# Attention weights turned by transposing DMA transfers instead of by TensorE, in a one-core hybrid encoder step

## The chip, the cores and the metric

The kernel runs on one core of a Trainium2 chip. The metric is the device time in microseconds (us). A kernel's time is the median of several runs. The profile comes from one execution of its own, and its span runs from the first to the last instruction.

## The reference, cut to what matters

One layer of a streaming encoder over 2048 prompt positions (and 32 sample positions): a combined projection, a short convolution, differential attention with 4 heads, an output projection, an MLP and a gate. The part that the change touches is the attention of the prompt:

```python
s = jnp.einsum('bqhmd,bkhmd->bhmqk', qf, kf)            # m = 0, 1: two maps per head
s = jnp.where(visible, s + bias[None, :, None], NEG_INF)
a = jax.nn.softmax(s, axis=-1)
attn = a[:, :, 0] - lam * a[:, :, 1]
o = jnp.einsum('bhqk,bkhd->bqhd', attn, v.astype(f))
o = rmsnorm(o, g_subln) * (1.0 - lam_init)
```

A block of 128 queries sees the keys up to its own block, so query block `qb` (0 to 15) has `qb + 1` key blocks of 128.

## The kernel before, in words

Every product is done in fp16 parts: a number is split into a high and a low fp16 part (`split`: ScalarE writes the high part, VectorE the low one), and three products are summed.

After the input has been normalised and turned, the attention runs head by head. A head's work is cut into 16 units (`Unit`), one for each query block, in ascending order for heads 0 to 2 and in descending order for head 3. A unit's keys are cut into chunks of up to 512 (`TG`). A unit has two stages:

- `scores`: for each of the two maps and each chunk TensorE makes the scores in one of three PSUM tiles (`sc`, L587 and L588), VectorE adds the position bias and keeps a running maximum (L591), and when the row is whole ScalarE takes the exponential and its sum (L598). The results are the fp32 tiles `s0` and `s1`, of which four lie in SBUF, for two units.
- `values`: ScalarE scales `s1` (L622), VectorE adds the maps (L105, `s<-s,sg,s`), TensorE transposes each 128x128 block in fp32 into PSUM (L629, `pta`), `split` makes two fp16 parts of it in `at` (three buffers), and TensorE multiplies them by the values in three products a block (L616 to L618, into `smb`). `subnorm` normalises the result.

`weave` writes one step: the scores of unit u, then `values` of the unit before it, and between the points of both a number of steps of `fill`, which are other heads' projections, the convolution, the sample attention and, in the last seven units of head 3, the first output projections. A scheduler then orders each engine's instructions by these priorities and sets the waits. All DMAs are issued by SyncE (SP), in order, and a queue's instruction waits there for its data, its buffer and one of eight completion counters.

After the attention come the output projection, the MLP and the gate, which the change does not touch.

Of the kernel before, what the change touches and what calls it, by code (L numbers as in the profile page):

```python
# [17 lines left out]
P = 128  # L18
# [16 lines left out]
def hymba_step_kernel(  # L35
# [34 lines left out]
    def small_o():  # L70
        k = turn["o"] = turn["o"] + 1
        return smb[:, (k % 4) * P:(k % 4 + 1) * P]
# [411 lines left out]
    def all_of(gen):  # L484
        for _ in gen:
            pass


    def weights_of(z1, z2, k0, rows=P):

        r, d, sg, sgc = t1("rz"), t1("ca"), t1("sg"), t1("sgc")
        ts(G, d[:rows], z1[:rows], alam[:rows], MUL, z2[:rows], ADD)
        V.reciprocal(out=r[:rows], in_=d[:rows])
        ts(G, sgc[:rows], z1[:rows], r[:rows], MUL, nlam[:rows], MUL)
        G.tensor_tensor(out=sg[:rows], in0=z2[:rows], in1=r[:rows], op=MUL)
        kk = t1("kk")
        if k0 is not None:
            ts(G, kk[:rows], sg[:rows], z1[:rows], MUL, k0[:rows], MUL)
        else:
            G.tensor_tensor(out=kk[:rows], in0=sg[:rows], in1=z1[:rows], op=MUL)  # L500
        ts(G, kk[:rows], kk[:rows], kk[:rows], MUL, EPS, MUL)
        return sg, sgc, kk

    def subnorm(o, kk, out, rows=P):
        jk = pq.tile([P, P], F16, tag="jko", bufs=1, name="jko")
        ss = t1("sso")
        A.activation(out=jk[:rows], in_=o, func=AF.Square, accum_out=ss[:rows])
        r = t1("rso")
        ts(G, r[:rows], ss[:rows], 1.0 / P, MUL, kk[:rows], ADD)
        G.tensor_tensor(out=r[:rows], in0=r[:rows], in1=mhalf[:rows], op=ALU.pow)  # L510
        ts(V, out, o, r[:rows], MUL)

    def sample_attention(j):
# [52 lines left out]
        T.transpose(pt[:, :DS], ys, ident[:DS, :DS])  # L566
        split(yas_h[:, j, :], yas_l[:, j, :], pt[:, :DS], gsa)

    class Unit:


        def __init__(self, j, qb, idx):
            self.idx = idx
            self.j, self.qb, self.nk = j, qb, (qb + 1) * P
            self.chunks = [(c, min(TG, self.nk - c)) for c in range(0, self.nk, TG)]

# [24 lines left out]
                    yield  # L601

        def weigh(self):
            self.sg, self.sgc, self.kk = weights_of(self.z[0], self.z[1], heads[self.j]["k0"])

        def values(self):
            s1, s2 = self.s
            vhl = heads[self.j]["vhl"]
            po = small_o()
            nkb = self.qb + 1  # L610

            def av(c0, w_, at):
                for i in range(w_ // P):
                    kb = c0 // P + i
                    a_ = slice(i * P, (i + 1) * P)
                    T.matmul(po, at[:, 0, a_], vhl[:, 0, kb], start=(kb == 0), stop=False)  # L616
                    T.matmul(po, at[:, 0, a_], vhl[:, 1, kb], start=False, stop=False)
                    T.matmul(po, at[:, 1, a_], vhl[:, 0, kb], start=False, stop=(kb == nkb - 1))  # L618

            for c0, w_ in self.chunks:  # L620
                cs = slice(c0, c0 + w_)
                A.activation(out=s2[:, cs], in_=s2[:, cs], func=AF.Copy, scale=self.sgc)  # L622
                stt(s1[:, cs], s1[:, cs], self.sg, s2[:, cs], MUL, ADD)
            yield
            ats = []
            for c0, w_ in self.chunks:
                pt = ptp.tile([P, TG], F32, tag="tp", name="pta")
                for i in range(w_ // P):
                    T.transpose(pt[:, i * P:(i + 1) * P], s1[:, c0 + i * P:c0 + (i + 1) * P], ident)  # L629
                at = att.tile([P, 2, TG], F16, tag="at", bufs=3, name="at")  # L630
                split(at[:, 0, :w_], at[:, 1, :w_], pt[:, :w_], 2.0 ** 14)
                ats.append((c0, w_, at))
                yield
                if len(ats) > 1:
                    av(*ats[-2])
            if len(self.chunks) == 1:
                yield
            av(*ats[-1])
            qi = self.qb % 4
            if self.idx % 4 == 0:  # L640
                yg_of[0] = att.tile([P, 4, P], F32, tag="yg", bufs=1, name="yg")
            self.yg = yg_of[0]
            subnorm(po, self.kk, self.yg[:, qi, :])

        def store(self):
            if self.idx % 4 != 3:
# [364 lines left out]
    all_of(run_chunk(GV, 0))  # L1011
    all_of(proj_q(0, 0))
    ready(place[GB, 0])
    last = before = None

    def weave(u, last, fills, nfill):

        points = len(u.chunks) * 2 if u else 0
        if last:
            points += len(last.chunks) + 1 + (len(last.chunks) == 1)  # L1020
        state = {"p": 0, "f": 0}

        def step():
            state["p"] += 1
            while state["f"] < nfill * state["p"] // points:
                state["f"] += 1
                for f in fills:
                    next(f, None)
        if u:
            for _ in u.scores():  # L1030
                step()
        if last:
            last.weigh()
            for _ in last.values():
                step()
        while state["p"] < points:
            step()

    for j in range(NH):
        set_bias(j)  # L1040
        fill = between(j)
        done = 0

        for idx in range(S // P):

            qb = idx if j < NH - 1 else S // P - 1 - idx
# [17 lines left out]
            weave(u, last, [fill], want - done)  # L1064
            done = want
            if idx % 4 == 3 and qfill is not None:
                all_of(qfill)
            if before:
                before.store()
            before, last = last, u  # L1070
        if j < NH - 1:
            all_of(fill)
    weave(None, last, [fill], EARLY_STEPS - done)
    before.store()
    last.store()
    all_of(fill)
# [690 lines left out]
```

## Time and profile before

| | |
|---|---|
| median of 3 runs | 2599.41 us (2597.41 to 2602.86) |
| profiled execution | 2600.33 us, span 2598.6 us |
| mean granted TensorE clock | 0.988 of full speed |
| TensorE busy (matmuls) | 2520.6 us, 97% |
| VectorE busy | 1677.6 us, 65% |
| ScalarE busy | 1208.8 us, 47% |
| GpSimd busy | 689.7 us, 27% |
| attention, from the first position bias to the last unit | about 97 to 960 us |

The matmuls are pipelined, so their durations overlap: what one costs is the time to the start of the next. The shares are means over stages with different limits.

### The profile page before, as it was taken

To read this page: it belongs to the slowest core of one execution; us is meant where nothing else is said; L and a number is where in the kernel's file an instruction comes from. 1 tells how busy PE (TensorE), PEld (TensorE's weight loads), DVE (VectorE), ACT (ScalarE), POOL (GpSimd) and SP (SyncE) were. 2 spreads that over 40 slices of the span, in tenths; PEclk is the share of its full clock that TensorE was granted. 3 is DMA by queue.
4 is the path that set the end of the run, shared out by engine and by line. 5 is a ranking of instruction groups with operands and counts; after the bars stand their busy time and mean duration, and the time that the engine had idled before them with its cause. 6 is when DMAs were issued, how large, how long until landed. Compare 5 with 4: busy or idle time off the path is not lost.

```text
span 2598.6 us, 42548 instructions
## 1 busy us (share of the span) xinstructions
PE 2520.6 (97%) x16495; PEld 1343.5 (52%) x16495; DVE 1677.6 (65%) x2873; ACT 1208.8 (47%) x2126; POOL 689.7 (27%) x1299
## 2 busy tenths in 40 slices
PE   8998999999999989999999999999999999999998
PEld 7755755765575554444444444444444444444444
DVE  6567957757877866875665656555455447655764
ACT  5446745644765555553444344345333223334553
POOL 2132233123222243432322222220120102223442
PEclk9999999999999999999999999999999999999999
DMA  5121111112120224554444444446653457531221
GB/s 176 50 66 33 43 30 46 42 34 58 45 57 27 82 78 134 171 201 171 157 166 164 163 157 167 142 162 245 225 206 118 158 174 251 201 114 59 86 79 57
DMA packets 213595, 311.57 MB, mean 120 GB/s; under 512 B 19024, under 2 KB 109552, under 8 KB 213392
## 3 DMA queue, kind: packets, MB, share of 16 engines
q1 hardware_dynamic: 213392, 308.85, 35.8%
q8 instruction: 129, 2.11, 0.3%
q14 instruction: 74, 0.61, 0.1%
HBM read 206.68 MB, written 97.92 MB: 117 GB/s over the span
## 4 chain that ended last, share of the span: by engine, by line
PE 66%; DVE 4%; ACT 2%; DMA 2%; issue 2%; POOL 1%; DVEq 0%; POOLq 0%; SPq 0%; ACTq 0%
PE mm L1299 8%; PE mm L1301 7%; PE mm L1300 7%; PE mm L1530 6%; PE mm L1532 6%; PE mm L1531 6%; PE mm L894 4%; PE mm L896 4%; PE mm L898 4%; PE lin L315 1%; PE lin L314 1%; PE lin L313 1%; DMA wtmp<-in_w_pe_gate_dram 1%; DVE s L591 1%; PE ptr L185 1%
## 5 line engine op out<-in xcount | busy, mean ns | idle before, releaser
L1530 PE MATMUL mm<-v,hl 128*128 128x512 f16 x896 | 339.8, 380 | 3.4 <-ACT hl L1491 3.4
L1532 PE MATMUL mm<-v,hl 128*128 128x512 f16 x896 | 340.0, 380 | 3.0 <-DVE hl L1492 3.0
L1531 PE MATMUL mm<-v,hl 128*128 128x512 f16 x896 | 340.6, 380 | 0.0
L313 PE MATMUL lin<-uh,whl 128*128 128x512 f16 (+1 forms) x832 | 264.4, 332 | 3.9 <-DVE ks L105 3.5
L314 PE MATMUL lin<-ul,whl 128*128 128x512 f16 (+1 forms) x832 | 264.4, 332 | 1.4 <-DVE ul L105 1.2
L315 PE MATMUL lin<-uh,whl 128*128 128x512 f16 (+1 forms) x832 | 264.1, 332 | 0.0
L1491 ACT ACTIVATE hl<-fr 128x1024 f16<-128x1024 f32 x112 | 116.9, 1051 | 302.1 <-PE mm L1532 287.7
L1492 DVE TENSOR_TENSOR hl<-fr,hl 128x1024 f16<-128x1024 f32 x112 | 145.1, 1306 | 171.8 <-ACT hl L1491 169.1
L598 ACT ACTIVATE s<-s,nm 128x128 f32<-128x128 f32 (+15 forms) x128 | 153.6, 1200 | 135.0 <-POOL nm L100 134.5
L1299 PE MATMUL mm<-u,w 128*128 128x512 f16 x448 | 170.5, 381 | 1.1 <-ACT w L170 1.1
L1300 PE MATMUL mm<-u,w 128*128 128x512 f16 x448 | 170.4, 380 | 0.0
L1300 PE MATMUL mm<-u2b,w 128*128 128x512 f16 x448 | 169.8, 379 | 0.0
L1301 PE MATMUL mm<-u,w 128*128 128x512 f16 x448 | 169.5, 381 | 0.0
L1299 PE MATMUL mm<-u2b,w 128*128 128x512 f16 x448 | 169.2, 379 | 0.0
L1301 PE MATMUL mm<-u2b,w 128*128 128x512 f16 x448 | 168.5, 379 | 0.0
L591 DVE CUSTOM_DVE_ANT_0 s<-sc,bias,mx 128x512 f32<-128x512 f32 (+3 forms) x192 | 134.9, 703 | 19.9 <-PE sc L588 15.5
L1530 PEld LDWEIGHTS <-hl 128*128 128x128 f16 x896 | 87.8, 98 | 113.6 <-issue 6.8
L1532 PEld LDWEIGHTS <-hl 128*128 128x128 f16 x896 | 87.7, 98 | 111.0 <-DVE hl L1492 5.4
L1301 PEld LDWEIGHTS <-w 128*128 128x128 f16 x896 | 87.9, 98 | 105.7 <-issue 0.8
L1531 PEld LDWEIGHTS <-hl 128*128 128x128 f16 x896 | 87.8, 98 | 104.3 <-issue 1.5
L1299 PEld LDWEIGHTS <-w 128*128 128x128 f16 x896 | 88.9, 99 | 100.5 <-ACT w L170 1.2
L1300 PEld LDWEIGHTS <-w 128*128 128x128 f16 x896 | 87.9, 98 | 98.9 <-issue 0.8
(451 smaller groups left out, 5981.9 us busy)
## 6 DMA issues: line engine op xcount, KB each, us to landing
ff_d<-e SPq DMA_DIRECT2D x224, 256.0 KB, 2.1
fr<-ff_d SPq DMA_DIRECT2D x112, 512.0 KB, 4.6
raw<-in_w_down_dram SPq DMA_DIRECT2D x80, 512.0 KB, 4.9
xt<-in_x_prompt_dram SPq DMA_DIRECT2D x32, 512.0 KB, 4.3
stg<-in_w_up_dram SPq DMA_DIRECT2D x16, 1024.0 KB, 6.5
stgd<-in_w_down_dram SPq DMA_DIRECT2D x16, 1024.0 KB, 5.6
stg<-in_w_in_dram SPq DMA_DIRECT2D x24, 512.0 KB, 4.1
h_d<-ht SPq DMA_DIRECT2D x16, 512.0 KB, 2.9
```

The costliest lines, as they stand in the source:

```text
L313: T.matmul(o, w[:, 0, ft], rh[:, ft, c], start=(ft == 0), stop=False)
L314: T.matmul(o, w[:, 0, ft], rl[:, ft, c], start=False, stop=False)
L315: T.matmul(o, w[:, 1, ft], rh[:, ft, c], start=False, stop=(ft == FT - 1))
L591: V.tensor_tensor_reduce(out=s_[:, c0:c0 + w_], in0=ps[:, :w_], in1=bias[:, b0:b0 + w_], scale=h["idd"], scalar=-BIG if prev is None else ...
L598: A.activation(out=s_[:, :nk], in_=s_[:, :nk], func=AF.Exp, bias=nm, accum_out=zz)
L1299: T.matmul(o, w[:, c, 0, kt], x[:, :, 0, kt], start=first and kt == 0, stop=False, skip_group_check=True)
L1300: T.matmul(o, w[:, c, 0, kt], x[:, :, 1, kt], start=False, stop=False, skip_group_check=True)
L1301: T.matmul(o, w[:, c, 1, kt], x[:, :, 0, kt], start=False, stop=kt == 3, skip_group_check=True)
L1492: V.tensor_tensor(out=hl[:, 1], in0=fr, in1=hl[:, 0], op=SUB)
L1530: T.matmul(ps, hl[:, 0, u % 2, c], v[:, 0], start=(u == 0), stop=False)
L1531: T.matmul(ps, hl[:, 0, u % 2, c], v[:, 1], start=False, stop=False)
L1532: T.matmul(ps, hl[:, 1, u % 2, c], v[:, 0], start=False, stop=(u == NU - 1))
```

## The change

For 57 of the 64 units (heads 0 to 2, and the first nine of head 3) the weights are turned by DMA. VectorE adds the maps without a scaling by ScalarE ahead of it (`weights_apart` gives the ratio `r`, with one reciprocal more), `split` makes the two fp16 parts before the turn, in place of `s1`, and one transposing DMA for each chunk, issued by SP, writes both parts turned into `at`. The products with the values move from the step after the scores to the step after that, and are woven with the scores of that step. The last seven units of head 3 keep the old way (`turn_and_values`). The transfers' targets come from two tags: `q4`, which had so far been used only later, and `at`.

```diff
+    def weights_apart(z1, z2, k0):
+        rd, d, r, sg, rz = t1("rz"), t1("ca"), t1("sgc"), t1("sg"), t1("rz2")
+        V.reciprocal(out=rz, in_=z2)
+        ts(G, r, z1, rz, MUL, nlam, MUL)
+        ts(G, d, z1, alam, MUL, z2, ADD)
+        V.reciprocal(out=rd, in_=d)
+        ts(G, sg, z2, rd, MUL, 2.0 ** 14, MUL)
...
         def __init__(self, j, qb, idx):
             self.idx = idx
+            self.by_dma = j < NH - 1 or idx < FAST[j]
+            self.even = Unit.count % 2 == 0
...
+        def turn(self):
+            s1, s2 = self.s
+            self.ats = []
+            for i, (c0, w_) in enumerate(self.chunks):
+                cs = slice(c0, c0 + w_)
+                stt(s1[:, cs], s2[:, cs], self.r, s1[:, cs], MUL, ADD)
+                hl = s2[:, cs].bitcast(F16)
+                split(hl[:, :w_], hl[:, w_:], s1[:, cs], self.sg)
+                if i < 2 or self.even:
+                    if i % 2 == 0:
+                        two = pmix.tile([P, 2, NH, 2, P], F16, tag="q4", bufs=3, name="at2")
+                    at = two[:, i % 2].rearrange("p a b c -> p (a b) c")
+                else:
+                    at = att.tile([P, 2, TG], F16, tag="at", bufs=3, name="at")
+                    at = at.rearrange("p a (b c) -> p (a b) c", c=P)
+                n = w_ // P
+                nc.sync.dma_start_transpose(out=at[:, :2 * n, :], in_=hl)
+                self.ats.append((c0, w_, at[:, :n, :], at[:, n:2 * n, :]))
+                yield
+        def products(self, c0, w_, hi, lo):
...
         def values(self):
+            for a in self.ats:
+                self.products(*a)
+                yield
+            self.normed()
...
+    def weave(u, last, before, fill, nfill):
+        parts = []
+        if u:
+            parts.append((u.scores(), 2 * len(u.chunks)))
+        if before and before.by_dma:
+            parts.append((before.values(), len(before.chunks)))
         if last:
+            last.weigh()
+            if last.by_dma:
+                parts.append((last.turn(), len(last.chunks)))
+            else:
+                parts.append((last.turn_and_values(), len(last.chunks) + 1 + (len(last.chunks) == 1)))
+        points = sum(n for _, n in parts)
...
+        if u and before and before.by_dma:
+            (a, na), (b, nb) = parts[:2]
+            parts = parts[2:]
+            for k in range(na + 1):
...
```

Three places show how it moves instructions. The first is TensorE in a unit of head 1 with nine key blocks, before. `pta` is a turned block, `s` a map, `lin` a projection that fills:

```order
L617 LDWEIGHTS at
L617 MATMUL smb<-vhl,at 128x128
L618 LDWEIGHTS at
L618 MATMUL smb<-vhl,at 128x128
L629 MATMUL pta<-ident,s_6859 128x128
L379 LDWEIGHTS ul
L379 MATMUL lin<-whl,ul 128x128
L377 LDWEIGHTS uh
```

The same engine in head 1 of the changed kernel, where the products of a unit begin (`at_6376` is written by DMA; L655 to L657 are the three products):

```order
L313 LDWEIGHTS whl
L313 MATMUL lin<-uh,whl 128x512
L359 MATMUL ptk<-ident,kf 128x128
L655 LDWEIGHTS at_6376
L655 MATMUL smb<-vhl,at_6376 128x128
L656 LDWEIGHTS at_6376
L656 MATMUL smb<-vhl,at_6376 128x128
```

No turned block stands among TensorE's rows of these units any more: 516 of the 544 are gone, and the products wait for a DMA in their first row of a chunk.

The second place is VectorE where head 0 ends and head 1 begins, before. `s_4669` and `s_4718` are the maps of the last unit of head 0, `s_4950` and `s_5140` belong to the first two units of head 1:

```order
L591 ISA s_4950,mx<-sc,bias,idd_2972 128x128
L591 ISA mx 128x1
L105 SCALAR_TENSOR_TENSOR s_4669<-s_4669,sg,s_4718 128x512 x2
L105 SCALAR_TENSOR_TENSOR at<-pta,at 128x384
L105 SCALAR_TENSOR_TENSOR s_4669<-s_4669,sg,s_4718 128x512 x2
L493 RECIPROCAL rz<-ca 128x1
L591 ISA s_5140,mx<-sc,bias,idd_2972 128x256
```

The same place in the changed kernel. `s_4513` and `s_4574` are the maps of the last unit of head 0; the rows that write `s_4574` make the low fp16 parts which the DMA reads; `s_4950`, of the second unit of head 1, takes over the buffer of `s_4574`:

```order
L105 SCALAR_TENSOR_TENSOR s_4513<-s_4574,sgc,s_4513 128x512 x4
L572 RECIPROCAL rz_4931<-z_4779 128x1
L575 RECIPROCAL rz<-ca 128x1
L105 SCALAR_TENSOR_TENSOR s_4574<-s_4513,sg,s_4574 128x512 x2
L100 TENSOR_SCALAR yg<-smb,rso 128x128
L105 SCALAR_TENSOR_TENSOR s_4574<-s_4513,sg,s_4574 128x512
L105 SCALAR_TENSOR_TENSOR s_4762<-s_4772,sgc,s_4762 128x128
L105 SCALAR_TENSOR_TENSOR s_4574<-s_4513,sg,s_4574 128x512
L105 SCALAR_TENSOR_TENSOR s_4772<-s_4762,sg,s_4772 128x128
L610 ISA s_4940,mx<-sc,bias,idd_2941 128x256
L610 ISA mx 128x1
L610 ISA s_4950,mx<-sc,bias,idd_2941 128x256
```

The low part is made from SBUF now instead of from PSUM, and the score row that writes `s_4950` has to wait for the transfers that read `s_4574`: the last of them can be issued only four rows earlier. This is the shortest such distance; within a head it is mostly 20 to 40 rows.

The third place is the queue of SP in head 1, before (`stg` are weights on their way in, `qs` the queries' parts, `cz`, `mixc_d` and `ya_d` results on their way out):

```order
L422 DMA qs<-qs 64x512
L424 DMA qs<-qs 64x512
L421 DMA qs<-qs 64x512
L423 DMA qs<-qs 64x512
L463 DMA out_dram<-cz 128x2x1
L464 DMA out_dram<-czs 128x2x1
L654 DMA ya_d<-yhl 128x4x256
```

The same queue, changed:

```order
L645 DMA_TRANSPOSE at_5687<-s_5468 128x8x128
L645 DMA_TRANSPOSE at_5687<-s_5468 128x4x128
L463 DMA out_dram<-cz 128x2x1
L464 DMA out_dram<-czs 128x2x1
L704 DMA ya_d<-yhl 128x4x256
L461 DMA mixc_d<-yt 128x512
L521 DMA sbig<-in_cache_k_dram 128x2x128
L522 DMA sbig<-in_cache_v_dram 128x2x128
L645 DMA_TRANSPOSE at_5844<-s_5612 128x8x128
L645 DMA_TRANSPOSE at_5844<-s_5612 128x6x128
```

The queue gains 150 rows, one to four for each unit, and they stand among the loads and stores that were there before.

## Rows read from the trace of the kernel before

**Rows 1.** The page, part 1: busy time, share of the span, instructions.
```profile
PE 2520.6 (97%) x16495; PEld 1343.5 (52%) x16495; DVE 1677.6 (65%) x2873; ACT 1208.8 (47%) x2126; POOL 689.7 (27%) x1299
```

**Rows 2.** Busy time in four stretches, one for each head.
```profile
core 0: us, PE busy (x) PEld busy (x) DVE busy (x) ACT busy (x) POOL busy (x), PEclk, DMA share, GB/s
97.00:315.00 218.00, 207.39 (x1980) 140.53 (x1978) 155.18 (x369) 123.73 (x240) 59.34 (x172) 0.99 0.18 51
315.00:526.00 211.00, 202.31 (x1691) 127.86 (x1688) 153.04 (x369) 117.47 (x229) 62.19 (x179) 0.98 0.14 39
526.00:742.00 216.00, 207.74 (x1713) 128.98 (x1711) 158.49 (x376) 117.68 (x231) 61.19 (x177) 0.98 0.18 49
742.00:960.00 218.00, 200.23 (x1537) 120.72 (x1534) 171.04 (x390) 125.06 (x240) 67.04 (x180) 0.98 0.18 56
sum 863.00, PE 817.67 PEld 518.09 DVE 637.76 ACT 483.94 POOL 249.76; mean PE 204.42 PEld 129.52 DVE 159.44 ACT 120.98 POOL 62.44
```

**Rows 3.** Waits of TensorE from 97 to 960 us: total, times, longest.
```profile
PE sc L587 <- DVE mx L591: 17.6, 20, 2.2
PE smb L616 <- ACT at L170: 4.0, 4, 1.5
PE smb L618 <- DVE at L105: 4.0, 6, 1.9
...
PE pta L629 <- DVE at L105: 1.3, 2, 1.0
...
PE pta L629 <- DVE s L105: 1.0, 1, 1.0
```

**Rows 4.** The group of TensorE's transposes: busy, mean ns; idle before.
```profile
L629 PE MATMUL pta<-ident,s 128*128 128x128 f32 x544 | 87.8, 280 | 5.0 <-DVE yhl L105 2.3 <-DVE at L105 1.3 <-DVE s L105 1.0
```

**Rows 5.** Timeline of TensorE around four transposes: start, duration.
```profile
274.19 0.22 PE L379 MATMUL lin<-whl,ul 128*128 128x128 f16 x1
274.25 0.61 PE L629 MATMUL pta<-ident,s 128*128 128x128 f32 x4
274.69 0.22 PE L377 MATMUL lin<-whl,uh 128*128 128x128 f16 x1
```

**Rows 6.** Groups of VectorE, shapes kept apart.
```profile
L105 DVE SCALAR_TENSOR_TENSOR s<-s,sg,s 128x512 f32<-128x512 f32 x112 | 80.5, 745 | 20.8 <-ACT s L622 18.1 <-POOL cz L433 1.4 <-POOL nm L100 1.1
L105 DVE SCALAR_TENSOR_TENSOR at<-pta,at 128x512 f16<-128x512 f32 x112 | 75.4, 682 | 2.4 <-ACT at L170 1.9
L105 DVE SCALAR_TENSOR_TENSOR v<-raw,swd,v 128x512 f16<-128x512 f32 x96 | 72.6, 797 | 3.2 <-ACT v L170 3.2
...
L493 DVE RECIPROCAL rz<-ca 128x1 f32<-128x1 f32 x64 | 10.2, 159 | 31.4 <-POOL ca L102 30.9
```

**Rows 7.** Groups of ScalarE, shapes kept apart.
```profile
L622 ACT ACTIVATE s<-s,sgc 128x512 f32<-128x512 f32 x112 | 74.3, 715 | 38.6 <-POOL sgc L102 38.1
L170 ACT ACTIVATE at<-pta 128x512 f16<-128x512 f32 x112 | 64.3, 590 | 39.5 <-PE pta L629 36.9 <-PE smb L618 1.6
...
L170 ACT ACTIVATE v<-raw,swd 128x512 f16<-128x512 f32 x96 | 63.4, 709 | 44.3 <-DVE raw L1470 25.0 <-DVE raw L1461 14.3 <-DMA raw<-in_w_down_dram 4.8
```

**Rows 8.** DMA issues by tile: count, KB each, median us to landing.
```profile
ff_d<-e SPq DMA_DIRECT2D x224, 256.0 KB, 2.1
...
u2b<-u_d SPq DMA_DIRECT2D x5, 1024.0 KB, 11.1
...
qs<-qs SPq DMA_DIRECT2D x64, 64.0 KB, 1.9
...
out_dram<-cz SPq DMA_DIRECT2D x4, 1.0 KB, 8.6
```

**Rows 9.** Timeline of SP in head 0: start, time to issue.
```profile
268.62 0.38 SPq L391 DMA_DIRECT2D out_dram<-vt  x1
269.58 0.47 SPq L422 DMA_DIRECT2D qs<-qs  x1
```

**Rows 10.** Busy time at the end of head 0, columns as in rows 2.
```profile
260.00:325.00 65.00, 64.71 (x783) 51.82 (x782) 58.84 (x140) 50.76 (x94) 19.23 (x55) 1.00 0.16 43
```

**Rows 11.** The same stretch, transposes of L629 alone: us, PE, PEld.
```profile
260.00:325.00 65.00, 10.87 (x70) 7.62 (x69) 1.00 0.16 43
```

More of the change, by code (lines that the diff above doesn't have):

```diff
@@ L603, in weigh @@
         def weigh(self):
+            if self.by_dma:
+                self.sg, self.r, self.kk = weights_apart(self.z[0], self.z[1], heads[self.j]["k0"])
+                return
             self.sg, self.sgc, self.kk = weights_of(self.z[0], self.z[1], heads[self.j]["k0"])
-        def values(self):
-            s1, s2 = self.s
[L608 to L618, printed above, removed]
+        def turn(self):
[17 more added lines that the diff above has]
+                yield
@@ new lines, in products, with normed @@
+        def products(self, c0, w_, hi, lo):
+            vhl = heads[self.j]["vhl"]
+            if c0 == 0:
+                self.po = small_o()
+            for i in range(w_ // P):
+                kb = c0 // P + i
+                T.matmul(self.po, hi[:, i, :], vhl[:, 0, kb], start=(kb == 0), stop=False)
+                T.matmul(self.po, hi[:, i, :], vhl[:, 1, kb], start=False, stop=False)
+                T.matmul(self.po, lo[:, i, :], vhl[:, 0, kb], start=False, stop=(kb == self.qb))
+        def normed(self):
+            if self.idx % 4 == 0:
+                yg_of[0] = att.tile([P, 4, P], F32, tag="yg", bufs=1, name="yg")
+            self.yg = yg_of[0]
+            subnorm(self.po, self.kk, self.yg[:, self.qb % 4, :])
@@ L631, in values @@
                 split(at[:, 0, :w_], at[:, 1, :w_], pt[:, :w_], 2.0 ** 14)
-                ats.append((c0, w_, at))
+                ats.append((c0, w_) + tuple(at[:, k, :w_].rearrange("p (i c) -> p i c", c=P) for k in range(2)))
                 yield
                 if len(ats) > 1:
-                    av(*ats[-2])
+                    self.products(*ats[-2])
             if len(self.chunks) == 1:
                 yield
[L638 to L643, printed above, removed]
+            self.products(*ats[-1])
+            self.normed()
         def store(self):
@@ L1013, in hymba_step_kernel @@
     ready(place[GB, 0])
-    last = before = None
-    def weave(u, last, fills, nfill):
-        points = len(u.chunks) * 2 if u else 0
-        if last:
-            points += len(last.chunks) + 1 + (len(last.chunks) == 1)
+    last = before = oldest = None
+    def weave(u, last, before, fill, nfill):
[4 more added lines that the diff above has]
+            parts.append((before.values(), len(before.chunks)))
+        if last:
+            last.weigh()
[4 more added lines that the diff above has]
+        points = sum(n for _, n in parts)
         state = {"p": 0, "f": 0}
@@ L1026, in step @@
                 state["f"] += 1
[L1027 to L1034, printed above, removed]
+                next(fill, None)
+        if u and before and before.by_dma:
+            (a, na), (b, nb) = parts[:2]
+            parts = parts[2:]
+            for k in range(na + 1):
+                if k < na:
+                    next(a, None)
+                    step()
+                else:
+                    all_of(a)
+                for _ in range(k * nb // na - (k - 1) * nb // na if k else 0):
+                    next(b, None)
+                    step()
+            all_of(b)
+        for g, _ in parts:
+            for _ in g:
                 step()
@@ L1063, in hymba_step_kernel @@
                 next(qfill, None)
-            weave(u, last, [fill], want - done)
+            weave(u, last, before, fill, want - done)
             done = want
@@ L1067, in hymba_step_kernel @@
                 all_of(qfill)
-            if before:
-                before.store()
-            before, last = last, u
+            for v in (oldest if oldest and oldest.by_dma else None, before if before and not before.by_dma else None):
+                if v:
+                    v.store()
+            oldest, before, last = before, last, u
         if j < NH - 1:
             all_of(fill)
-    weave(None, last, [fill], EARLY_STEPS - done)
+    weave(None, last, before, fill, EARLY_STEPS - done)
     before.store()
```

7 lines of the change are left out of this document (added).

## The prediction

> **What bounds the kernel now.** I read the page first, then the attention alone, since nothing else changes. The page shows TensorE busy 97% of the span [rows 1], but that is a mean over the whole program and counts the overlapping tails of short matmuls. So I cut the attention into one stretch for each head: TensorE is busy 817.7 of 863 us there, VectorE 637.8 (74%), ScalarE 483.9 (56%), and the DMA engines are at 14 to 18% [rows 2]. TensorE is the bound, with VectorE the next. The clock is granted at 0.98 to 0.99 in all four stretches, so it is at its upper level and has nothing to give back.
>
> The waits say what TensorE lacks when it does stop. The largest wait is 17.6 us for VectorE's bias rows: the three score tiles are full and TensorE can't write a fourth. The waits that belong to the turning and to its products are small: 4.0 and 4.0 us for the two fp16 parts, 1.3 and 1.0 us ahead of the transposes, together 10.3 us [rows 3]. So what the change can give is TensorE's own time on the transposes, and what it can spoil is VectorE's lead on the scores.
>
> **The change part by part.**
>
> *Transposes removed.* 57 units go by DMA. In heads 0 to 2 they have 136 key blocks each, in head 3 (16 blocks down to 8) 108: 516 of the 544 transposes. The group shows 87.8 us busy and 280 ns each [rows 4], but both count tails that lie over the next instruction. The price is read where a group of four stands between other matmuls: it starts at 274.25 and the next matmul at 274.69, so 0.44 us for four, 0.110 us each [rows 5]. 516 x 0.110 = 56.8 us. The far end is the group's busy time, 87.8/544 = 0.161 us each, 83 us; I take 56.8, since only that time is free for another matmul.
>
> [...]
>
> *Waits at the transposes and products.* The products come a unit later, so the fp16 parts should be there when TensorE gets to them: the 10.3 us go, if the transfer is in time (below). The other end is that they only change their name: 0.
>
> *VectorE.* For each chunk the adding of the maps stays (745 ns at 512 columns). The low part is made from fp32 in SBUF instead of from PSUM. The nearest row to that is the weights' split, `v<-raw`: 797 against 682 ns [rows 6], 115 ns more. The units have 108 chunks of 512 and 14 each of 128, 256 and 384, which I price by width: 108 x 0.115 + 42 x 0.057 = 14.8 us. One reciprocal more in each unit is 57 x 0.159 = 9.1 us [rows 6]. Together 23.9 us on an engine with 225 us of idle time in these stretches [rows 2]. Bounds: 0, if all of it falls into idle time; 23.9, if all of it delays scores that TensorE waits for. I take the whole, because VectorE's scores are TensorE's largest wait and the turn now stands in one piece behind the scores of each step, where VectorE has work and TensorE has only fill.
>
> *ScalarE.* The scaling of `s1` goes (715 ns at 512) and the high part costs 709 instead of 590 ns [rows 7]: about 0.6 us less for each full chunk, some 80 us in all on an engine that isn't the bound. I count nothing. The other end is the 18.1 us that VectorE waits for the scaled map [rows 6], which could come back as earlier scores.
>
> *The transfers.* 150 transposing DMAs, up to 256 KB each (128 partitions x 1024 fp16). The trace has none, so landing and issue are bounded by other rows. For landing, the near rows are 256 KB stores (2.1 us) and the copies from SBUF to SBUF (64 KB, 1.9 us); far off stands the slowest bulk load, 11.1 us [rows 8]. Two readers wait for them. The products stand on TensorE a whole step behind the turn. VectorE overwrites the buffer of `s1` two units later; 20 to 40 of its rows lie between, half of them at about 0.7 us, so some 10 us. Below that a landing is hidden. Only where a head begins are there four to a dozen rows, 1 to 5 us: perhaps 12 units in all. At 2 to 3 us this costs nothing; at 11.1 us those 12 units would wait some 7 us each and the others about 1 us, up to 130 us on VectorE, about half of it over its idle time. I take the near end and 0, and keep +60 us for the range.
>
> On SP an issue takes 0.38 to 0.47 us [rows 9]. 150 x 0.47 = 70 us are spread over 860, on a queue that has little else. Behind a transpose that waits for its split stand weight loads, query copies and stores; the loads are asked for a chunk ahead, so a microsecond there is covered by the projections.
>
> *The sum.* 2600.3 (the profiled execution) - 56.8 - 10.3 + 23.9 = 2557.1 us. The median of the runs lies 0.9 us below that execution, so 2556 us, 1.7% faster.
>
> **The rivals.**
>
> *A. VectorE takes over as the bound in the long units.* At the end of head 0, where the units are longest, VectorE is busy 58.8 of 65 us beside a TensorE at 64.7 [rows 10], in a stretch with 70 transposes [rows 11]. Its own share of the 23.9 us, 70/516, is 3.2 us, which makes 62 of 65: nothing to gain there. If so in all units of nine and more blocks (100 of a head's 136), only 26% of the 56.8 us stay, 15 us, and the small waits stay too: 2599.4 - 15 = 2585 us. For it speaks the wait of 17.6 us; against it that VectorE is at 71 to 78% over each head [rows 2], and that the fill can be moved between units only as far as the order allows.
>
> *B. The waits only move.* TensorE waits for the transfers about as long as it saved. 57 units need to wait 0.75 us each on average to eat the 43 us. The time is then that of before, 2599 us. The product's place a step later speaks against it; the short distances at the head's beginnings speak for it.
>
> *C. The transposing transfers are the bound, and the kernel is slower.* All go through one queue in order, and that order also holds every load and store. The 516 blocks are 129 transfers of full size. Taking the forecast's 818 us for the attention and leaving 90 us for some 200 other issues at 0.45 us, the point is (818 - 90)/129 = 5.6 us for each: above that, SP or the DMA engines are later than TensorE. At 6.2 us the attention takes 129 x 6.2 + 90 = 890 us, plus 20 us for what then stands still at the head's ends: 2599 + 47 = 2646 us. For it: the landing of 1 KB in short elements takes 8.6 us [rows 8], so a transfer whose pieces are small can be far slower than its bytes. Against it: the plain copies inside SBUF, 1.9 us.
>
> [...]
>
> **How the numbers follow.** Within 0.2% (5 us) a measurement of this kernel can't be told from no change. The forecast has 0.45, A 0.16, B 0.10, C 0.29 (nothing in the trace shows such a transfer, so the side with the open price gets nearly a third). The forecast and A are faster: 0.61; B is the same: 0.10; C is slower: 0.29. The likeliest case's own range is 2535 to 2578: down by the ScalarE end and part of the VectorE end, up by half of the transposes. For 8 in 10 the range takes in A, B and C up to 2650, and leaves out the worse half of C: 2534 to 2650 us.
>
> **What would show it.** Right: no L629 rows in heads 0 to 2, the attention's end near 917 us instead of 960; the transposing transfers land in under 5 us; TensorE's wait for VectorE's bias rows grows by less than 24 us; VectorE's low part near 797 ns. Wrong: waits of TensorE's products or of VectorE's bias rows for the transfers of tens of us (B); VectorE at 90% and TensorE's wait at the scores twice as long (A); SP or a DMA share near full in the long units, and issues of several us each (C). The prediction fails most easily on the price of a transposing transfer, and next on whether VectorE's extra time meets its idle time.

## The result, and the profile after

The changed kernel takes 2561.93 us (median of 4 runs, 2560.36 to 2562.13), the kernel before, run beside it, 2601.14 us (4 runs). The ratio is 0.9849, 95% interval 0.9832 to 0.9866: 39.2 us or 1.5% faster. Forecast were 2556 us and 43 us. The profiled execution has a span of 2560.1 us, against 2598.6.

Page of the changed kernel, part 1 and the line on DMA packets; they answer to [rows 1]:

```profile
PE 2464.4 (96%) x15979; PEld 1286.8 (50%) x15979; DVE 1691.2 (66%) x2930; ACT 1138.2 (44%) x1976; POOL 747.8 (29%) x1299
DMA packets 350489, 345.35 MB, mean 135 GB/s; under 512 B 155920, under 2 KB 246448, under 8 KB 350288
```

TensorE has 56 us less, VectorE 13.6 us more, ScalarE 71 us less. GpSimd takes 58 us more for the same 1299 instructions; from 97 to 940 us an instruction takes 436 ns on average (311.8 us for 715), before 353 (237.4 for 672). With plain copies (below) it is 433 (314.8 for 727), so the turning isn't the reason, and the cause is open. Busy time in four stretches over the attention, columns as in [rows 2]:

```profile
97.00:309.00 212.00, 204.76 (x1938) 132.24 (x1936) 163.25 (x397) 110.01 (x210) 72.14 (x174) 1.00 0.41 92
309.00:513.00 204.00, 195.49 (x1694) 119.23 (x1692) 166.56 (x410) 107.53 (x213) 88.66 (x199) 1.00 0.47 92
513.00:709.00 196.00, 180.16 (x1514) 108.89 (x1513) 150.56 (x364) 92.98 (x171) 66.22 (x156) 0.97 0.42 88
709.00:915.00 206.00, 178.00 (x1236) 99.91 (x1234) 164.06 (x383) 101.85 (x192) 77.99 (x173) 0.93 0.40 96
sum 818.00, PE 758.41 PEld 460.27 DVE 644.42 ACT 412.37 POOL 305.02; mean PE 189.60 PEld 115.07 DVE 161.11 ACT 103.09 POOL 76.25
```

The stretches, whose ends are set by eye, are 45 us shorter in sum. TensorE's busy time falls by 59.3 us in them and by 56.2 over the whole run, and its idle time grows, from 863 - 817.7 = 45.3 to 818 - 758.4 = 59.6 us. The DMA engines' share has gone from 0.14 to 0.18 up to 0.40 to 0.47. The granted clock is lower in the last two stretches than before (0.97 and 0.93 against 0.98).

Where the attention ends, by the first and last start of the bias rows and of the last product (source view; before and after):

```profile
L591 DVE DVE_READ_ACCUMULATOR2_ANT mx<- x320: 71/82/86, 147.9 to 954.2; 128x1 f32 x160
L618 PE MATMUL smb<-vhl,at x544: 216/219/314, 160.7 to 976.8; 128*128 128x128 f16 x182
```

```profile
L610 DVE DVE_READ_ACCUMULATOR2_ANT mx<- x320: 71/82/86, 148.0 to 910.7; 128x1 f32 x160
L657 PE MATMUL smb<-vhl,at x544: 216/219/315, 162.5 to 939.6; 128*128 128x128 f16 x182
```

The last bias row is 43.5 us earlier, the last product 37.2, the span's end 38.5. So nearly the whole gain is made in the attention, and some 6 us are given back in its last units.

What TensorE waits for in the attention (total, times, longest), which answers to [rows 3]:

```profile
PE sc L606 <- DVE mx L610: 18.3, 21, 3.1
PE lin L313 <- DVE yt L105: 14.0, 4, 7.9
PE smb L655 <- DVE yg L100: 9.6, 2, 8.2
PE smb L655 <- DMA at<-s: 6.9, 11, 1.1
```

Of the four small waits of before at the transposes and products, 0.8 us are left, in the units that keep the old way. The wait at the scores is as it was in sum (18.3 against 17.6), but it has moved: in heads 0 to 2 it fell from 12.0 to 6.3 us, in head 3 it rose from 5.5 to 12.0. New are 6.9 us for the transfers and two waits of some size: for the convolution's `yt` and for the normalised row `yg` (1.2 us before).

The transfers and VectorE's low part, in the DMA issues by tile (count, median us to landing), the source view of the issuing line (ns, least/median/most) and VectorE's groups:

```profile
at<-s SPq DMA_TRANSPOSE x150, 3.2
L645 SPq DMA_TRANSPOSE at<-s x150: 1167/1257/2707, 157.2 to 874.2; - x150
L105 DVE SCALAR_TENSOR_TENSOR s<-s,sg,s 128x512 f16<-128x512 f32 x108 | 77.4, 741 | 7.1 <-ACT s L170 7.0
L105 DVE SCALAR_TENSOR_TENSOR s<-s,sgc,s 128x512 f32<-128x512 f32 x108 | 75.9, 746 | 5.0 <-POOL sgc L102 4.5
```

A transfer lands in 3.2 us, the median of all 150, of which 108 have 256 KB; this counts from the start of its issue. The issue takes SP 1.26 us of it, nearly three times the 0.38 to 0.47 us of a plain transfer [rows 9]. The low part takes 741 ns, against 682 from PSUM [rows 6].

### The profile page after: what moved, and what is told of

The parts are those of the page before. It is cut to its first block, busy times and chain, and to the rows that moved or that the text cites. A ratio compares the mean times of both kernels' runs of the same rounds, so it can differ in the third digit from the quotient of the medians.

```text
span 2560.1 us, 41714 instructions
## 1 busy us (share of the span) xinstructions
PE 2464.4 (96%) x15979; PEld 1286.8 (50%) x15979; DVE 1691.2 (66%) x2930; ACT 1138.2 (44%) x1976; POOL 747.8 (29%) x1299
## 2 busy tenths in 40 slices
DMA packets 350489, 345.35 MB, mean 135 GB/s; under 512 B 155920, under 2 KB 246448, under 8 KB 350288
## 4 chain that ended last, share of the span: by engine, by line
PE 64%; DVE 5%; DMA 3%; issue 2%; POOL 1%; ACT 1%; DVEq 0%; SPq 0%; POOLq 0%; ACTq 0%
PE mm L1368 8%; PE mm L1370 7%; PE mm L1369 7%; PE mm L1599 6%; PE mm L1601 6%; PE mm L1600 6%; PE mm L944 5%; PE mm L946 5%; PE mm L948 5%; DVE s L105 1%; PE lin L313 1%; PE lin L314 1%; PE lin L315 1%; DVE s L610 1%; PE ptr L185 1%
```

## The experiments

Every time is a median. The kernel before had 2600.7 to 2602.0 us beside them, so the times can be set against 2561.9 for the change. Each puts one question to a term of the sum.

**The TensorE work put back.** The 516 transposes run again as work that nobody reads; all else is the changed kernel.

```diff
+                pt = ptp.tile([P, TG], F32, tag="tp", name="pta")
+                for b in range(w_ // P):
+                    T.transpose(pt[:, b * P:(b + 1) * P], s1[:, c0 + b * P:c0 + (b + 1) * P], ident)
```

> The changed kernel with the 516 transposes put back on TensorE as work that nobody reads (from the added maps into PSUM), beside the transfers. The theory: TensorE's time is the bound, so most of 516 x 0.110 = 56.8 us comes back, 2600 to 2620 us. The rival (the gain is in the chain through ScalarE and PSUM that the change takes away, not in TensorE's time): under 2580 us.

Measured: 2621.05 us, 59.1 us over the change, 0.115 us for each transpose. That is near the distance to the next start (0.110 us, [rows 5]) and far from the row's duration of 0.28 us. The saving of 56.8 us stands. It is a net price: other waits shift in this kernel (the one for `yg` is 5.2 us against 9.6), so a few of the 59.1 us may be theirs.

**The delay alone.** Products one unit later, but weights still scaled by ScalarE and turned by TensorE.

```diff
+                A.activation(out=s2[:, cs], in_=s2[:, cs], func=AF.Copy, scale=self.sgc)
+                stt(s1[:, cs], s1[:, cs], self.sg, s2[:, cs], MUL, ADD)
...
+                    T.transpose(pt[:, b * P:(b + 1) * P], s1[:, c0 + b * P:c0 + (b + 1) * P], ident)
...
-                nc.sync.dma_start_transpose(out=at[:, :2 * n, :], in_=hl)
+                ptr = pt[:, :w_].rearrange("p (b c) -> p b c", c=P)
+                split(at[:, :n, :], at[:, n:2 * n, :], ptr, 2.0 ** 14)
```

> The delay alone: the products come one unit later, as in the changed kernel, but the weights are still scaled on ScalarE and turned by TensorE in fp32. The theory (TensorE's time on the transposes is what is gained, the delay only spares the small waits): 2585 to 2600 us, since at most the 10.3 us of small waits can go. The rival (the delay is what gains, because the products no longer wait for their parts): about 2565 us.

Measured: 2617.57 us, ratio 1.0061 (1.0049 to 1.0074): slower by 16 us, and both expectations missed. TensorE's waits of this kernel:

```profile
PE pta L636 <- DVE at L105: 12.7, 7, 4.5
PE sc L606 <- DVE mx L610: 9.7, 13, 1.9
PE pta L636 <- DVE yhl L105: 4.9, 1, 4.9
```

The scores wait less (9.7 against 17.6 us), but all of a unit's transposes now stand in a row, with no products between them, and wait for VectorE to empty their PSUM tiles: 12.7 us where it was 1.3. The delay is no gain in itself. How the 16 us add up isn't shown: with the turning left on TensorE, the delay also changes the order of its work.

**The transfers without the delay.** The DMA turn, and the products in the same step as before.

```diff
-        if before and before.by_dma:
-            parts.append((before.values(), len(before.chunks)))
...
                 parts.append((last.turn(), len(last.chunks)))
+                parts.append((last.values(), len(last.chunks)))
...
```

> The transfers alone: the weights are turned by DMA as in the changed kernel, but the products stand in the same step as the turn, as before. The theory: TensorE waits for the transfers (1.25 us of issue and 3.2 us to land) in most of the 57 units, some 1 to 3 us each, so 60 to 150 us of the gain are lost again and the kernel is slower than before: 2620 to 2700 us. The rival (the scheduler covers the landing with the fill): about 2562 us, as the changed kernel.

Measured: 2574.89 us, ratio 0.9895 (0.9882 to 0.9909). The transfers bring 27 us without the delay, and the delay 13 more on top of them. The theory missed by far. The waits say why it is no more:

```profile
PE sc L606 <- DVE mx L610: 23.4, 18, 9.2
PE smb L655 <- DMA at<-s: 17.7, 19, 4.2
```

The products wait 17.7 us for transfers, not 6.9. Even in one step, then, most of the landings, 3.3 us for each of 150 transfers, lie under other work that TensorE has in hand.

**Plain copies for transposing transfers.** The same bytes go by plain transfers inside SBUF, so the weights are not turned.

```diff
-                nc.sync.dma_start_transpose(out=at[:, :2 * n, :], in_=hl)
+                nc.sync.dma_start(out=at[:, :2 * n, :], in_=hl.rearrange("p (b c) -> p b c", c=P))
```

> The changed kernel with plain copies of the same bytes in place of the transposing transfers (the weights are then not turned). It prices what the transposing costs over a copy: 0.47 us to issue and about 2 us to land instead of 1.25 and 3.2. The theory (TensorE waits 6.9 us for the transfers and the queue of SP holds some stores up): 2 to 15 us less, 2547 to 2560 us. The rival (the transfers are hidden): 2560 to 2564 us.

Measured: 2551.99 us, ratio 0.9814 (0.9799 to 0.9829): the turning of the transfers costs 9.9 us. The runs lie between 2543.67 and 2555.24, so the size is rough. In the DMA issues and the source view of this kernel:

```profile
at<-s SPq DMA_DIRECT2D x108, 256.0 KB, 2.3
L645 SPq DMA_DIRECT2D at<-s x150: 464/476/2573, 157.2 to 858.4; - x150
```

It lands 0.9 us sooner, and 0.78 of this is the issue: SP issues it in 0.48 us and not in 1.26. Behind the issue a transposing transfer takes 3.2 - 1.26 = 1.9 us and a plain one 2.3 - 0.48 = 1.8.

**Two transfers for each chunk.** The high and the low part go apart, 300 issues for the same bytes.

```diff
-                nc.sync.dma_start_transpose(out=at[:, :2 * n, :], in_=hl)
+                nc.sync.dma_start_transpose(out=at[:, :n, :], in_=hl[:, :w_])
+                nc.sync.dma_start_transpose(out=at[:, n:2 * n, :], in_=hl[:, w_:])
```

> Two transposing transfers per chunk, one for each part, 300 instead of 150, the same bytes. Theory (what the transfers cost, 10 us against plain copies, goes by bytes, and SP has room for 150 more issues): 2558 to 2570 us. Rival (it goes by the time SP takes to issue one, 1.25 us each, which the loads and stores behind them wait for): 2572 to 2600. Under 2555 would say that the smaller transfer lands so much earlier that the last products of a unit start sooner.

Measured: 2580.91 us, 19.0 us over the change, in the rival's range. DMA issues, source view, and a wait of TensorE and one of VectorE:

```profile
at<-s SPq DMA_TRANSPOSE x300, 2.4
L646 SPq DMA_TRANSPOSE at<-s x150: 1146/1216/2421, 159.9 to 901.8; - x150
PE smb L658 <- DMA at<-s: 12.4, 11, 2.4
DVE s L610 <- DMA at<-s: 11.5, 5, 4.4
```

Each transfer lands sooner (2.4 us) and issuing one takes as long as before (1.2 us). What grew is SP's time: 150 x 1.21 = 182 us more for 19.0 us of the kernel's time, 0.10 us per us. By that rate the 150 x 0.78 = 117 us that plain copies spare SP are worth 12 us, near the 9.9 measured. So the price goes with the number of issues and not with the bytes. It is paid through the landing, though: a chunk's second transfer is issued behind its first, so the chunk is whole about 1.2 + 2.4 = 3.6 us after the first issue began, and not 3.2. L658, the product that reads the second transfer, waits 12.4 us, and VectorE's score rows wait 11.5 us for buffers where it was 2.9. Whether the loads and stores behind the issues lose as well, as the rival has it, wasn't separated.

**Transfers issued by ScalarE.**

```diff
-                nc.sync.dma_start_transpose(out=at[:, :2 * n, :], in_=hl)
+                nc.scalar.dma_start_transpose(out=at[:, :2 * n, :], in_=hl)
```

> The 150 transposing transfers are issued from ScalarE's queue and not from SP's. Theory (the 1.25 us of issue and the wait for VectorE's split are harmless on SP, which computes nothing, and would stop ScalarE's exponentials and copies behind them: 150 x 1.25 = 188 us on an engine busy 412 of 818): 2585 to 2640 us. Rival (transfers that wait at the head of SP's queue hold back loads and stores, and that is what the change still loses): under 2556 us.

Measured: 2585.61 us, 23.7 over the change, at the near end of the theory's range: on SP the issue stands in nobody's way but that of other transfers, on ScalarE it stands ahead of exponentials. TensorE's wait at the scores is 24.5 us, and VectorE's score rows wait 19.0 us for the transfers to free their buffers, against 18.3 and 2.9; what the exponentials alone lose wasn't measured. The queue of these transfers stands alone here, in part 3 of the page (packets, MB, share of 16 engines):

```profile
q10 hardware_dynamic: 136896, 33.84, 7.6%
```

33.84 MB in 136,896 packets is 247 bytes each. The page of the changed kernel has just so many packets under 512 B more than that of before, 155,920 against 19,024. The page of before:

```profile
DMA packets 213595, 311.57 MB, mean 120 GB/s; under 512 B 19024, under 2 KB 109552, under 8 KB 213392
```

**More VectorE work.** One more operation per chunk, the combined map times 1.0.

```diff
+                ts(V, s1[:, cs], s1[:, cs], 1.0, MUL)
                 split(hl[:, :w_], hl[:, w_:], s1[:, cs], self.sg)
```

> One more VectorE operation per chunk in front of the split: the combined map multiplied in place by 1.0, 108 of 512 columns and 42 narrower, between 0.4 and 0.75 us each by the nearest rows, 50 to 95 us of VectorE in all. Theory (VectorE, busy 644 us of 818 in the attention, has slack, and a microsecond more on it costs TensorE a third or less): 2570 to 2592 us. Rival, the prediction's own rule (VectorE's added time counts in full): 2610 to 2655 us. No change at all, 2558 to 2566, would say that the 23.9 us booked for VectorE should have been nothing.

Measured: 2603.23 us, 41.3 us over the change. The page's part 1 for this kernel, and the added operations in VectorE's groups:

```profile
PE 2484.3 (95%) x15979; PEld 1295.8 (50%) x15979; DVE 1736.3 (67%) x3080; ACT 1139.1 (44%) x1976; POOL 769.0 (30%) x1299
L100 DVE TENSOR_SCALAR s<-s 128x512 f32<-128x512 f32 x108 | 41.6, 415 | 0.1
L100 DVE TENSOR_SCALAR s<-s 128x384 f32<-128x384 f32 x14 | 5.0, 360 | 0.0
L100 DVE TENSOR_SCALAR s<-s 128x256 f32<-128x256 f32 x14 | 3.9, 282 | 0.0
L100 DVE TENSOR_SCALAR s<-s 128x128 f32<-128x128 f32 x14 | 3.0, 216 | 0.0
```

The rows come to 53.5 us, 0.77 us of the kernel's time for each. But VectorE's rows overlap at their ends, as TensorE's do (in the changed kernel a row of 0.75 us starts at 564.70 us and the next at 565.37): its busy time over the run grew by only 1736.3 - 1691.2 = 45.1 us, and by that measure a microsecond costs 0.92, nearly the prediction's whole and far more than the theory's third. An engine that is busy 644 of 818 us sets most of the pace for work that stands between the scores and the products.

**Less VectorE work.** The low part of every second chunk by GpSimd, after ScalarE has scaled the map.

```diff
-                split(hl[:, :w_], hl[:, w_:], s1[:, cs], self.sg)
+                if i % 2:
+                    A.activation(out=s1[:, cs], in_=s1[:, cs], func=AF.Copy, scale=self.sg)
+                    A.activation(out=hl[:, :w_], in_=s1[:, cs], func=AF.Copy, scale=1.0)
+                    G.tensor_tensor(out=hl[:, w_:], in0=s1[:, cs], in1=hl[:, :w_], op=SUB)
+                else:
+                    split(hl[:, :w_], hl[:, w_:], s1[:, cs], self.sg)
```

> The low part of every second chunk (61 of 150) is taken by GpSimd, as a difference of the scaled map, which ScalarE scales in place first, and the high part: 61 x 0.74 = 45 us less on VectorE, some 61 x 0.72 = 44 us more on ScalarE, some 61 x 1.3 to 1.75 = 80 to 107 us more on GpSimd, by its groups of 128x512 subtractions. Theory (a microsecond of VectorE is worth what the doubled cost showed, 41.3 / 53.5 = 0.77, and the two other engines have room): 2520 to 2540 us. Rival (GpSimd's small operations, the negated maxima and the factors, then stand behind subtractions, and the low part lands later): 2555 to 2600.

Measured: 2576.23 us, 14.3 over the change: the rival. GpSimd's group and VectorE's remaining low parts:

```profile
L639 POOL TENSOR_TENSOR s<-s,s 128x512 f16<-128x512 f32 x40 | 52.0, 1301 | 39.6 <-ACT s L638 37.6 <-DVE s L105 1.2 <-DVE mx L610 0.7
L105 DVE SCALAR_TENSOR_TENSOR s<-s,sg,s 128x512 f16<-128x512 f32 x68 | 58.7, 873 | 9.3 <-ACT s L170 8.9 <-POOL iw L102 0.4
```

GpSimd stands 37.6 us at the head of its queue for ScalarE's scaled map, and its queue also holds the negated maxima that the exponentials need. VectorE's remaining low parts average 873 ns against 741, so the 40 of full width that left it, 29.6 of the 45 us counted on, made their group only 18.7 us shorter (58.7 against 77.4). TensorE's wait at the scores grows from 18.3 to 28.1 us. The price of work added to VectorE is no price of work taken off it: here that was lost again on two engines in the same chain.

**Head 3 back on TensorE.**

```diff
-            self.by_dma = j < NH - 1 or idx < FAST[j]
+            self.by_dma = j < NH - 1
```

> The nine units of head 3 that the change turned by transfers go back to TensorE (scaled by ScalarE, turned in fp32, values in the same unit); heads 0 to 2 stay as changed. Theory (a transpose taken off TensorE is worth its 0.115 us wherever it stands): 108 of them come back, +12.4 us, less some of the 13.5 us that TensorE waits in head 3 for yt and for yg: 2564 to 2574 us. Rival (in head 3 the waits behind the new form eat what it saves, the change there is worth nothing): 2555 to 2562.

Measured: 2567.59 us, ratio 0.9874 (0.9852 to 0.9897). The changed units of head 3 are worth some 5.7 us, where their 108 transposes are worth 12.4; the interval touches that of the change, so the size is rough. The waits in head 3 show what the change gives back there: the one for `yg` is 9.6 us with it and 1.3 without, the one for `yt` 3.9 and none, the one at the scores 12.0 and 3.7. A stretch of 65 us around the wait for `yg`, first of before, then of the change, then of this kernel (columns as in [rows 2]):

```profile
886.00:951.00 65.00, 51.01 (x377) 31.02 (x377) 56.12 (x132) 47.07 (x97) 30.21 (x79) 0.95 0.23 71
```

```profile
845.00:910.00 65.00, 47.70 (x325) 30.48 (x325) 55.17 (x132) 44.11 (x90) 31.84 (x78) 0.82 0.34 87
```

```profile
847.00:912.00 65.00, 52.72 (x380) 33.20 (x381) 55.95 (x130) 47.46 (x103) 30.70 (x79) 0.91 0.19 59
```

With the change TensorE is idle longest there, and the clock granted is lowest, 0.82.

**Three tries at the two new waits.** The first: the convolution's stores (`mixc_d<-yt`) issued by ScalarE, out of SP's queue.

```diff
-            st(out=mixc_d[j, :, cols(tg)], in_=o)
+            A.dma_start(out=mixc_d[j, :, cols(tg)], in_=o)
```

> One line: the 16 stores of the finished convolution (mixc_d<-yt, line 461) are issued from ScalarE's queue and not from SP's, where they stand behind transposing transfers that wait for VectorE. Theory (SP's queue, blocked at its head by a transfer whose input is not ready, holds back the store, the store holds the tile yt, and TensorE's 14.0 us of waiting at lin for VectorE's yt come from it): these 14.0 us go and little takes their place, 2546 to 2556 us, and the wait lin<-yt is under 4 us. Rival (that wait is VectorE's own lag, the store only comes last by the record): 2558 to 2566, and the wait stays at 10 us or more.

Measured: 2560.18 us, no change, and TensorE still waits 13.4 us for `yt`. The theory fell. The trace of the changed kernel then showed another cause: VectorE, in order, stands at the maximum of a weight load, and TensorE's projections wait behind it (timelines of VectorE and TensorE):

```profile
581.60 1.22 DVE L140 TENSOR_REDUCE am<-stg 128x1 f32<-128x1024 f32 x1 [12.06 <-DMA stg<-in_w_in_dram]
583.92 0.75 DVE L105 SCALAR_TENSOR_TENSOR yt<-lin,iw,yt 128x512 f32<-128x512 f32 x1
584.72 0.58 PE L313 MATMUL lin<-uh,whl 128*128 128x512 f16 x1 [7.88 <-DVE yt L105]
```

The clock is low beside this wait too. TensorE stood still for 7.9 us, and in the 3.9 us behind that the granted clock is 0.52 and products of 512 columns start 0.43 us apart; from 588.6 to 592.4 us it is 1.00 again, and they start 0.22 us apart. Whether the wait brought the lower clock wasn't tested. The 3.9 us, columns as in [rows 2]:

```profile
584.70:588.60 3.90, 3.88 (x15) 1.64 (x14) 3.74 (x8) 0.53 (x2) 0.94 (x2) 0.52 0.53 134
```

SP had issued that load at 566.7 us, between two stores of 1 KB in short elements, and it took 14.9 us; a median load takes 3.9. So the second try took these stores out of SP's queue.

```diff
-            st(out=conv_prompt[0, 0][:, j * P:(j + 1) * P].rearrange("w p -> p w"), in_=cz[0][:, S:S + 2])
-            st(out=conv_sample[0, 0][:, j * P:(j + 1) * P].rearrange("w p -> p w"), in_=cz[1][:, DS:DS + 2])
+            A.dma_start(out=conv_prompt[0, 0][:, j * P:(j + 1) * P].rearrange("w p -> p w"), in_=cz[0][:, S:S + 2])
+            A.dma_start(out=conv_sample[0, 0][:, j * P:(j + 1) * P].rearrange("w p -> p w"), in_=cz[1][:, DS:DS + 2])
```

> The eight 1 KB stores of the convolution's tail (out_dram<-cz and out_dram<-czs, lines 463 and 464) are issued from ScalarE's queue and not from SP's. In the changed kernel a 512 KB load of input weights issued at 566.7 us, 2 us behind one of these stores, lands at 581.6, 14.9 us later, where the median load takes 3.9; VectorE stands at its head for 12.1 us, and TensorE for 7.9 us at lin for VectorE's yt. Theory (the load is held up in SP's queue by the small store ahead of it, and the wait lin<-yt in head 2 is this load's lateness): the load lands in under 6 us, that wait falls from 10.1 to under 3 us, 2549 to 2556 us. Rival (the transfers compete wherever they are issued, or what VectorE is spared it waits elsewhere): 2558 to 2566.

Measured: 2562.59 us, no change. In its DMA issues from 545 to 600 us:

```profile
stg<-in_w_in_dram SPq DMA_DIRECT2D x2, 512.0 KB, 9.9
out_dram<-cz ACTq DMA_DIRECT2D x1, 1.0 KB, 11.6
out_dram<-czs ACTq DMA_DIRECT2D x1, 1.0 KB, 14.5
```

The small stores still take 12 to 15 us, and of the two loads one takes 4.0 and one 15.8. The queue is not what holds the load. Nor is the turning: in the kernel with plain copies, which has no transposing transfer, the load in head 2 takes 15.2 us beside the same two stores, and in the kernel before a store of 256 KB beside them takes 9.8 us, where its median is 2.3 (DMA issues from 560 to 561 us and from 606 to 607 us):

```profile
stg<-in_w_in_dram SPq DMA_DIRECT2D x1, 512.0 KB, 15.2
```

```profile
ya_d<-yhl SPq DMA_DIRECT2D x1, 256.0 KB, 9.8
```

In the changed kernel's attention seven other transfers take over 7 us, and each of the seven is in flight with one of these 1 KB stores. In the kernel before it is two, but none of its weight loads is in flight with one (its slowest takes 5.4 us). So the change met an old hazard: it moved a load, on which VectorE waits, beside the stores. No run takes the stores away, so what the meeting costs the kernel isn't measured.

The third: the split of the output weights, a pile of 9.8 us on VectorE ahead of `yg`, with one more empty step behind each row.

```diff
             split(w[:, 0], w[:, 1], out_scale["sgs"][r], out_scale["aswo" if r < 4 else "swo"])
             yield
+            yield
...
-    NEARLY, EARLY_STEPS = 2, 28
+    NEARLY, EARLY_STEPS = 2, 36
```

> The eight rows of the output weights, split late in head 3 (9.8 us of VectorE from 856.4 to 866.8 and 8.5 us of ScalarE in the trace of the changed kernel, right ahead of the low parts and of the row yg that TensorE waits 8.2 us for), are spread over twice as many steps: one more empty step behind each, 36 steps instead of 28 in the seven units. Theory (this pile-up is what head 3 loses, by the wait of 8.2 us and by the clock of 0.82 granted in 845 to 910): 2548 to 2556 us, with the longest wait for yg under 3 us and a higher clock there. Rival (the wait moves to the next thing that these rows push back): 2558 to 2568.

Measured: 2562.40 us, and the wait for `yg` still 8.2 us. But the edit did not spread the rows. The source view of the tile in this kernel:

```profile
L105 DVE SCALAR_TENSOR_TENSOR w<-wst,i_wo,w x4: 1275/1276/1277, 856.8 to 861.1; 128x1024 f16<-128x1024 f32 x4
L105 DVE SCALAR_TENSOR_TENSOR w<-wst,aswo,w x4: 1275/1276/1276, 862.3 to 865.9; 128x1024 f16<-128x1024 f32 x4
```

They stand within half a microsecond of where they were, probably because all become ready at once, when their scale is known. So this run doesn't test the pile-up. The timelines of the changed kernel show what stands in the wait all the same (VectorE, VectorE, TensorE, and the busy times from 856 to 867 us):

```profile
861.97 4.86 DVE L105 SCALAR_TENSOR_TENSOR w<-wst,aswo,w 128x1024 f16<-128x1024 f32 x4
868.07 0.34 DVE L100 TENSOR_SCALAR yg<-smb,rso 128x128 f32<-128x128 f32 x1
868.46 0.26 PE L655 MATMUL smb<-vhl,at 128*128 128x128 f16 x1 [8.17 <-DVE yg L100]
856.00:867.00 11.00, 1.23 (x5) 0.38 (x4) 11.00 (x14) 9.93 (x15) 4.25 (x4) 0.75 0.01 3
```

VectorE is busy all of these 11 us, mostly with the eight rows, and TensorE 1.2 us. The same eight rows stand together in the kernel before (from 897.8 us) and in the one with head 3 on TensorE (from 854.7), and there TensorE's longest wait beside them is 2.3 us. So it is the rows and the new form together: what TensorE has next in the changed kernel waits behind them. A run in which the rows are really spread is missing, so how much they cost is open.

## Why the prediction was right, step by step

**Transposes, -56.8 us.** Right: 59.1 by the work put back, 56.2 by TensorE's busy time over the run. A row lasts 280 ns, but that is no price: a transpose in a stream costs 0.115 us.

**Waits at the transposes and products, -10.3 us.** These waits went, as said. What the step left out is that others came: 6.9 us for transfers, and more at `yt` and `yg`, which aren't at the turn at all.

**VectorE, +23.9 us.** The price was nearly right, the amount was not. The low part is 741 ns and not 797, and VectorE's busy time grew by 13.6 us over the whole run. A microsecond of it counts 0.92, by the run with more VectorE work, where the prediction took 1: 13.6 x 0.92 = 12.5 us. The prediction's sign, that TensorE's wait at the scores grows by less than 24 us, came true (0.7 us), but it says little: VectorE's price shows in that wait only in part. With the added VectorE work the wait grew by 15.5 us, to 33.8, and the kernel by 41.3.

**Transfers, 0.** Undersized. The landing was about right (3.2 us against 2 to 3 taken), and TensorE's 6.9 us and VectorE's 2.9 us of waiting for it are small. The issue was wrong: 1.26 us was counted as 0.47, and transposing costs 9.9 us against plain copies. The halves of the run with two transfers land 0.8 us sooner than the whole (2.4 us against 3.2), by an estimate from that 128 KB in 0.8 us or 160 GB/s. Behind the issue a transposing transfer takes about as long as a plain one, 1.9 us against 1.8; with the issue it doesn't, 3.2 against 2.3.

**ScalarE, 0.** Right. It is busy 71.6 us less in the stretches. Whether that is why the wait at the scores fell in heads 0 to 2 wasn't tested; in sum that wait didn't fall.

**The sum.** With the measured terms it is -59.1 - 10.3 + 12.5 + 9.9 = -47.0 us, against 39.2 measured. The 7.8 us between them have no run of their own, nor has what the plain copies themselves cost. The two new waits (7.9 us in head 2 behind the late load, 8.2 us in head 3) and the lower clock beside them are large enough for it. They can't be added in full, since the terms come from kernels in which these waits differ too: with the added VectorE work the longest wait for `yt` is 2.2 us and the longest for `yg` 3.4. That the forecast's 43 us came so close is in part luck: two errors, too much for VectorE and nothing for the transfers and their side effects, nearly cancel. The same holds for TensorE's idle time: the forecast had it grow by 23.9 - 10.3 = 13.6 us, and it grew by 14.3, but out of other waits.

Two figures of the prediction don't follow from its terms: half of the transposes would raise the likeliest case to 2556 + 28 = 2584 us and not to 2578, and the forecast's attention is 820 us and not 818. Neither enters the forecast of 2556 us.

**The rivals.** A, VectorE as the bound, would have given 2585 us: VectorE isn't full over the head (79%), but its price of 0.92 says that much of A's reasoning was right. B fell: the waits for the transfers are 6.9 us and not 43. C needed 5.6 us for each transfer on SP; they take 1.3 us to issue and 3.2 us to land.

**The delay.** The prediction counted on it to hide the landing, and that is what it does: 13 us with transfers, and a loss of 16 us without them.

Open are what the late load in head 2 and the pile-up of weight splits in head 3 cost the kernel, each by itself.

## What to carry to other kernels

Price work taken off a pipelined engine by the distance between starts, not by the rows' durations: here 0.11 us against 0.28, and the run with the work put back agrees with the former. The same goes for VectorE: 53.5 us of added rows were 45.1 us of its time. Put a measured price on each microsecond of the engine next to the bound; "it has 20% idle time" would have made it free, and it cost 0.92. When a transfer replaces an engine's work, ask for the issue as well as for the landing: with two transfers of half the size each landed sooner, a whole chunk later, and the kernel was 19 us slower. And look at what a new order puts side by side: small stores in short elements and a pile of weight splits, both there before, came to stand ahead of TensorE's work.

## What the runs showed of the hardware that was not expected

- Issuing a transposing DMA takes SP 1.26 us at the median, a plain one of the same bytes 0.48 us, and it hardly depends on the size (1.22 us for half the bytes).
- A transposing transfer inside SBUF goes in packets of 247 bytes on average, and still lands up to 256 KB in 3.2 us at the median, 0.9 us behind a plain copy, of which 0.78 us are the issue.
- A store of 1 KB in short elements (two of them are 544 packets) takes 8 to 17 us in the attention, and transfers in flight with it can be as late: a 512 KB load that takes 3.9 us as a rule took 14.9 to 15.8, with transposing transfers or with plain ones, and with the stores in either queue.
